# Channel-major matmuls that walk the tokens from the last to the first

## The chip, the cores and the metric

The kernel runs on one core of a Trainium2 chip. The metric is the device time of one execution in microseconds (us); before and after are timed in turn on the same chip. The engines are named as in the profile: PE is the matmul engine (TensorE), PEld its weight loads, DVE is VectorE, ACT is ScalarE, POOL is GpSimd, SP is the queue that issues most of the loads.

## What is computed

One layer of a hybrid encoder block on 256 tokens with 2048 channels, all in float32:

```
n = rms_norm(h, norm_mix_w)
proj = einsum("bsd,dp->bsp", n, w_in)          # 2048 -> 13344 channels
out_a = delta_mixer(...)                       # gated DeltaNet, both directions
out_b = dilated_mixer(...)                     # windowed attention, three dilations
h = h + einsum("bsm,md->bsd", concat(out_a, out_b), w_out)
n = rms_norm(h, norm_ffn_w)
up = depthwise_conv(einsum("bsd,df->bsf", n, w_ffn_in), conv_ffn_w)   # 2048 -> 11264
h = h + einsum("bsf,fd->bsd", silu(gate) * val, w_ffn_out)            # 5632 -> 2048
out = rms_norm(h, norm_final_w)
```

## The kernel before, in words

Nearly all the work is in four large matrix products. Each float32 weight is split into a rounded part `hi` (ACT, line 265) and a remainder `lo` (DVE, line 266), both of the type float32r, and the activations are kept in the same way as a pair. A product is then three matmuls that add into one bank of PSUM: hi by high, hi by low, lo by high. The weights come in pieces of 1 MB over SP's queue into four buffers (`raws`), are split into four buffers (`his`, `los`), and each split piece is one item of a list that `run_items` works off in order; the smaller work of the layer (convolutions, DeltaNet, attention) is dealt out between the items by `pump`.

Where a result is wanted with channels on the partitions and tokens along the row ("channel-major"), `cm_block` makes it: the query, key, value and z projections of DeltaNet, the queries and keys of attention, and the whole up projection of the MLP. The weights are the stationary operand, 128 x 128; the moving operand is a row of `xcat`, which for each of 16 groups of 128 channels holds 256 tokens of the high part and then 256 tokens of the low part, contiguous in SBUF. Each of the 168 blocks of 128 output channels makes 16 x 3 matmuls of 256 columns into columns 0 to 255 of one bank (lines 314, 315 and 316, 2688 matmuls each). When the last has finished, one instruction reads the bank: `evac` on ACT (line 329), or for the up projection a multiplication on DVE (line 1375).

The other large products use the activations as the stationary operand and the weights as the moving one: `v_slab` (lines 382 to 384, 256 columns) and `tm_group` for the two output projections (lines 1224 to 1226, 512 columns). They do not go through `cm_block`.

A few instructions elsewhere touch memory in another order than ascending and contiguous, and the rows below show them. `evac(natural(pad))` and lines 1203 and 1204 write with a step of four elements (16 bytes); line 1204 also reads one operand so. Line 861 reads 2048 elements of the tile `W` from the last to the first (steps of -64 and -1). Line 763, on POOL, runs four times for each head; two of the four write 64-element runs in descending order (the second and the third), the other two in ascending order.

Of the kernel before, what the change touches and what calls it, by code (L numbers as in the profile page):

```python
# [11 lines left out]
T = 256  # L12
D = 2048
KT = D // P
# [71 lines left out]
def block_kernel(tc, A, out, dbg=None):  # L86
# [7 lines left out]
    mm = nc.tensor.matmul  # L94
# [9 lines left out]
    def aview(t, off, dims):  # L104

        return bass.AP(tensor=t.tensor, offset=t.offset + off, ap=[list(t.ap[0])] + [list(d) for d in dims])
# [41 lines left out]
    xcat = xp.tile([P, KT, 512], F32R, name="xcat")  # L148
# [150 lines left out]
    def next_acc():  # L299
        accn[0] += 1  # L300
        return accs[accn[0] % len(accs)]

    def cm_block(ch, j, done, width=P):

        box = {}

        def half(kh):
            def mms(hi, lo):
                if kh == 0:
                    box["acc"] = next_acc()  # L310
                acc = box["acc"][:width, :T]
                for kk in range(8):
                    k = kh * 8 + kk
                    mm(acc, lhsT=hi[:, kk, :], rhs=xcat[:, k, :T], start=k == 0, stop=False)  # L314
                    mm(acc, lhsT=hi[:, kk, :], rhs=xcat[:, k, T:], start=False, stop=False)  # L315
                    mm(acc, lhsT=lo[:, kk, :], rhs=xcat[:, k, :T], start=False, stop=k == KT - 1)  # L316

            return mms

        for kh in range(2):  # L320
            Item(ch[kh], lambda t, j=j: t[:, :, j * width : (j + 1) * width], half(kh),
                 (lambda: done(box["acc"])) if kh else None, AT_CM)
# [129 lines left out]
    for k2 in range(8):  # L452
        bk = DB.get()
        for e in range(2):
            k = 2 * k2 + e
# [4 lines left out]
        for e in range(2):  # L460
            k = 2 * k2 + e
            src = bk[:, e * T : (e + 1) * T]
            ACT(xcat[:, k, :T], src, AF.Copy, scale=nw_mix[:, k : k + 1])
        for e in range(2):
            k = 2 * k2 + e
# [1019 lines left out]
```

## Time and profile before

| what | value |
|---|---|
| median of 3 runs | 1547.11 us (1544.25 to 1547.69) |
| the profiled execution, its own time | 1545.1 us |
| its span, first to last instruction | 1543.3 us |
| mean granted clock of PE | 0.997 of full speed |
| PE busy | 98% of the span |
| DVE, ACT, POOL busy | 67%, 54%, 11% |

The profile is of one execution. Its own time is 1.8 us above its span and 2.0 us below the median of the three runs.

### The profile page before, as it was taken

Reading aid. Unit: us, or ns where it says so; the run is one execution under the profiler, and the core shown is the slowest. Engines: PE = TensorE matmul, PEld = TensorE weight load, DVE = VectorE, ACT = ScalarE, POOL = GpSimd, SP = SyncE. Lnnn points to the kernel's source line nnn. Section 1 sums busy time; section 2 is a strip of 40 time slices with the busy share of each in tenths; the row PEclk is TensorE's granted clock in tenths of the full one; section 3 lists DMA queues with packets and bytes.
Section 4 is the critical chain, followed back from the end, with each engine's and each line's share of the span. In section 5 each row is a group of like instructions: output and inputs, shape, how many; then the busy total and the mean of one; then the engine's idle time right before and its main releaser. Section 6 shows DMA issues by size and latency. Waiting matters only on the chain.

```text
span 1543.3 us, 28173 instructions
## 1 busy us (share of the span) xinstructions
PE 1514.2 (98%) x11531; PEld 1443.4 (94%) x11531; DVE 1039.9 (67%) x1703; ACT 827.9 (54%) x1430; POOL 164.5 (11%) x245
## 2 busy tenths in 40 slices
PE   7999998999999999999999999999999999999997
PEld 7999998999999999997889999999999999888886
DVE  5878976979864666665557767677676676455454
ACT  5598874545555646554555544544544544344342
POOL 3264552000012202100000000000000000000000
PEclk9999999999999999999999999999999999999999
DMA  9656789646558636634765555565655657566552
GB/s 255 219 184 223 233 294 214 203 145 204 183 142 258 206 122 204 199 124 151 272 217 184 173 191 192 172 209 167 198 185 179 203 165 260 197 210 207 191 191 82
DMA packets 247283, 301.20 MB, mean 195 GB/s; under 512 B 10981, under 2 KB 207766, under 8 KB 246770
## 3 DMA queue, kind: packets, MB, share of 16 engines
q1 hardware_dynamic: 235602, 269.81, 54.4%
q0 software_dynamic: 11120, 29.01, 6.1%
q8 instruction: 90, 1.47, 0.4%
q10 hardware_dynamic: 432, 0.59, 0.1%
q14 instruction: 39, 0.32, 0.1%
HBM read 285.69 MB, written 13.65 MB: 194 GB/s over the span
## 4 chain that ended last, share of the span: by engine, by line
PE 91%; DMA 3%; ACT 2%; issue 2%; DVE 1%; POOL 1%; POOLq 0%; SPq 0%; ACTq 0%; DVEq 0%
PE bank L314 19%; PE bank L316 19%; PE bank L315 19%; PE bank L1224 7%; PE bank L1225 7%; PE bank L1226 7%; PE bank L382 3%; PE bank L383 3%; PE bank L384 3%; DMA raw<-in_w_in_dram 1%; PE bank L978 1%; PE bank L1024 1%; ACT hi L265 1%; PE bank L1019 1%; ACT kb L748 1%
## 5 line engine op out<-in xcount | busy, mean ns | idle before, releaser
L266 DVE TENSOR_TENSOR lo<-raw,hi 128x1024 fp32r<-128x1024 f32 x504 | 619.3, 1230 | 399.9 <-ACT hi L265 397.5
L265 ACT ACTIVATE hi<-raw 128x1024 fp32r<-128x1024 f32 x504 | 533.5, 1060 | 548.7 <-PE bank L315 262.5
L314 PE MATMUL bank<-xcat,hi 128*128 128x256 f32 x2688 | 758.4, 282 | 5.4 <-ACT qk L329 5.1
L315 PE MATMUL bank<-xcat,hi 128*128 128x256 f32 x2688 | 751.8, 280 | 0.0
L316 PE MATMUL bank<-xcat,lo 128*128 128x256 f32 x2688 | 751.6, 280 | 0.0
L314 PEld LDWEIGHTS bank<-xcat,hi 128*128 128x128 f32 x2688 | 506.2, 188 | 8.4 <-ACT qk L329 5.5
L315 PEld LDWEIGHTS bank<-xcat,hi 128*128 128x128 f32 x2688 | 512.0, 190 | 0.0
L316 PEld LDWEIGHTS bank<-xcat,lo 128*128 128x128 f32 x2688 | 505.6, 188 | 0.0
L1226 PE MATMUL bank<-hi,gtl 128*128 128x512 f32 x336 | 130.7, 389 | 0.0
L1225 PE MATMUL bank<-lo,gth 128*128 128x512 f32 x336 | 130.7, 389 | 0.0
L1224 PE MATMUL bank<-hi,gth 128*128 128x512 f32 x336 | 130.7, 389 | 0.0
L382 PE MATMUL bank<-hi,xcat 128*128 128x256 f32 x384 | 109.2, 284 | 0.0
L384 PE MATMUL bank<-hi,xcat 128*128 128x256 f32 x384 | 106.9, 278 | 0.0
L383 PE MATMUL bank<-lo,xcat 128*128 128x256 f32 x384 | 106.8, 278 | 0.0
L1224 PEld LDWEIGHTS bank<-hi,gth 128*128 128x128 f32 x336 | 63.1, 188 | 13.2
L1226 PEld LDWEIGHTS bank<-hi,gtl 128*128 128x128 f32 x336 | 63.1, 188 | 13.1
L1225 PEld LDWEIGHTS bank<-lo,gth 128*128 128x128 f32 x336 | 63.1, 188 | 13.0
L382 PEld LDWEIGHTS bank<-hi,xcat 128*128 128x128 f32 x384 | 72.4, 188 | 0.5
L384 PEld LDWEIGHTS bank<-hi,xcat 128*128 128x128 f32 x384 | 72.5, 189 | 0.0
L383 PEld LDWEIGHTS bank<-lo,xcat 128*128 128x128 f32 x384 | 72.3, 188 | 0.0
L1388 DVE SCALAR_TENSOR_TENSOR fy<-fpad,cwf,fy 128x256 f32<-128x256 f32 x132 | 63.4, 480 | 2.3
L1418 POOL DMA_DIRECT2D nfb<-in_norm_final_w_dram x1 | 0.6, 585 | 485.7 <-PE bank L316 485.7
(299 smaller groups left out, 1439.2 us busy)
## 6 DMA issues: line engine op xcount, KB each, us to landing
raw<-in_w_in_dram SPq DMA_DIRECT2D x104, 1024.0 KB, 5.7
raw<-in_w_ffn_in_dram SPq DMA_DIRECT2D x88, 1024.0 KB, 5.2
raw<-in_w_ffn_out_dram SPq DMA_DIRECT2D x44, 1024.0 KB, 5.0
raw<-in_w_out_dram SPq DMA_DIRECT2D x14, 1024.0 KB, 5.1
rec_d<-rec POOLq DMA_DIRECT2D x8, 768.0 KB, 7.1
rr<-rec_d POOLq DMA_DIRECT2D x6, 512.0 KB, 4.7
xt<-in_x_dram SPq DMA_DIRECT2D x4, 512.0 KB, 8.4
gam<-cg_d POOLq DMA_DIRECT2D x8, 256.0 KB, 8.7
```

Of the source, the lines that this page charges most:

```text
L265: ACT(hi, src, AF.Copy)
L266: V.tensor_sub(lo, src, hi.bitcast(F32))
L314: mm(acc, lhsT=hi[:, kk, :], rhs=xcat[:, k, :T], start=k == 0, stop=False)
L315: mm(acc, lhsT=hi[:, kk, :], rhs=xcat[:, k, T:], start=False, stop=False)
L316: mm(acc, lhsT=lo[:, kk, :], rhs=xcat[:, k, :T], start=False, stop=k == KT - 1)
L382: mm(o, lhsT=xh, rhs=hi[:, kk, :], start=k == 0 and t == 0, stop=False, skip_group_check=True)
L383: mm(o, lhsT=xh, rhs=lo[:, kk, :], start=False, stop=False, skip_group_check=True)
L384: mm(o, lhsT=xl, rhs=hi[:, kk, :], start=False, stop=k == KT - 1, skip_group_check=True)
L1224: mm(a[t], lhsT=xh, rhs=hi[:, kk, :], start=st, stop=False)
L1225: mm(a[t], lhsT=xh, rhs=lo[:, kk, :], start=False, stop=False)
L1226: mm(a[t], lhsT=xl, rhs=hi[:, kk, :], start=False, stop=sp_)
L1388: stt(y, pad[:, d : d + T], cwf[:, d, b : b + 1], y, op0=ALU.mult, op1=ALU.add)
```

## The change

In `cm_block` alone, both token axes are turned round. The accumulator's view starts at column 255 and steps by -1; the two views of `xcat` start at token 255 and step by -1. The moving operand is thus read from the last token to the first, and the sum is written from the last column to the first, so that each token still lands in its own column. `aview` builds an access pattern from a tile, an offset and pairs of step and count. The weights, the order of the three matmuls, the banks and the readers of the banks stay as they are. Two lines are added, so that all later line numbers grow by 2.

```
             def mms(hi, lo):
                 if kh == 0:
                     box["acc"] = next_acc()
-                acc = box["acc"][:width, :T]
+                acc = aview(box["acc"][:width], T - 1, [[-1, T]])
                 for kk in range(8):
+
                     k = kh * 8 + kk
-                    mm(acc, lhsT=hi[:, kk, :], rhs=xcat[:, k, :T], start=k == 0, stop=False)
-                    mm(acc, lhsT=hi[:, kk, :], rhs=xcat[:, k, T:], start=False, stop=False)
-                    mm(acc, lhsT=lo[:, kk, :], rhs=xcat[:, k, :T], start=False, stop=k == KT - 1)
+                    xh, xl = [aview(xcat[:, k, :], o + T - 1, [[-1, T]]) for o in (0, T)]
+                    mm(acc, lhsT=hi[:, kk, :], rhs=xh, start=k == 0, stop=False)
+                    mm(acc, lhsT=hi[:, kk, :], rhs=xl, start=False, stop=False)
+                    mm(acc, lhsT=lo[:, kk, :], rhs=xh, start=False, stop=k == KT - 1)
```

## Rows read from the trace of the kernel before

**Rows 1.** The page's first part: busy time, share, instructions of each engine.
```profile
PE 1514.2 (98%) x11531; PEld 1443.4 (94%) x11531; DVE 1039.9 (67%) x1703; ACT 827.9 (54%) x1430; POOL 164.5 (11%) x245
```

**Rows 2.** The page's fourth part: the chain that ended last, by engine and line.
```profile
PE 91%; DMA 3%; ACT 2%; issue 2%; DVE 1%; POOL 1%; POOLq 0%; SPq 0%; ACTq 0%; DVEq 0%
PE bank L314 19%; PE bank L316 19%; PE bank L315 19%; PE bank L1224 7%; PE bank L1225 7%; PE bank L1226 7%; PE bank L382 3%; PE bank L383 3%; PE bank L384 3%; DMA raw<-in_w_in_dram 1%; PE bank L978 1%; PE bank L1024 1%; ACT hi L265 1%; PE bank L1019 1%; ACT kb L748 1%
```

**Rows 3.** Matmuls by line and shape: count, busy us, mean ns, idle before.
```profile
L314 PE MATMUL bank<-xcat,hi 128*128 128x256 f32 x2688 | 758.4, 282 | 5.4 <-ACT qk L329 5.1 <-ACT pad L329 0.2
L315 PE MATMUL bank<-xcat,hi 128*128 128x256 f32 x2688 | 751.8, 280 | 0.0
L316 PE MATMUL bank<-xcat,lo 128*128 128x256 f32 x2688 | 751.6, 280 | 0.0
L1226 PE MATMUL bank<-hi,gtl 128*128 128x512 f32 x336 | 130.7, 389 | 0.0
...
L1198 PE MATMUL bank<-PT,vv 128*128 128x128 f32 x64 | 8.4, 275 | 0.0
...
L1195 PE MATMUL bank<-PT,vv 128*128 128x256 f32 x32 | 8.2, 378 | 0.0
```

**Rows 4.** Four stretches: length, busy us (count) of PE, PEld, DVE, ACT, POOL, PEclk, DMA.
```profile
346.00:384.00 38.00, 38.00 (x338) 38.00 (x337) 35.17 (x46) 21.86 (x35) 0.00 (x0) 1.00 0.66 209
900.00:938.00 38.00, 38.00 (x325) 38.00 (x325) 26.65 (x40) 19.80 (x29) 0.00 (x0) 1.00 0.62 201
1000.00:1100.00 100.00, 100.00 (x851) 100.00 (x851) 70.26 (x105) 49.41 (x70) 0.00 (x0) 1.00 0.58 190
1300.00:1400.00 100.00, 100.00 (x443) 82.81 (x442) 49.79 (x47) 41.74 (x43) 0.70 (x1) 1.00 0.64 216
```

**Rows 5.** ACT by line and shape: ascending, contiguous copies, and one with 16-byte steps.
```profile
L265 ACT ACTIVATE hi<-raw 128x1024 fp32r<-128x1024 f32 x504 | 533.5, 1060 | 548.7 <-PE bank L315 262.5 <-PE bank L1226 158.9 <-issue 63.8
...
L329 ACT ACTIVATE qk<-bank 128x256 f32<-128x256 f32 x48 | 17.8, 370 | 0.0
...
L329 ACT ACTIVATE pad<-bank 128x256 f32<-128x256 f32 x19 | 11.9, 624 | 0.1
...
L425 ACT ACTIVATE g_hi<-g_raw 128x512 fp32r<-128x512 f32 x1 | 0.6, 609 | 0.0
```

**Rows 6.** ACT's line 861, the descending read: ns min/median/max, first and last start.
```profile
L861 ACT ACTIVATE tm<-W x1: 1911/1911/1911, 449.8 to 449.8; 64x2048 f32<-64x2048 f32 x1
```

**Rows 7.** DVE by line and shape: a contiguous subtraction and one with 16-byte steps.
```profile
L1403 DVE TENSOR_TENSOR gtl<-fy,gth 128x256 fp32r<-128x256 f32 x22 | 9.1, 415 | 0.5 <-ACT gth L1402 0.5
...
L1204 DVE TENSOR_TENSOR mxl<-bank,mxh 128x256 fp32r<-128x256 f32 x8 | 5.1, 639 | 17.5 <-ACT mxh L1203 17.5
```

**Rows 8.** POOL's line 763 in four stretches: first ascending, second descending, twice.
```profile
101.20:101.70 0.50, 0.45 (x1) 1.00 0.49 51
101.70:102.25 0.55, 0.46 (x1) 1.00 0.82 136
202.00:202.51 0.51, 0.45 (x1) 1.00 1.11 353
202.51:203.10 0.59, 0.45 (x1) 1.00 1.15 356
```

**Rows 9.** DVE's line 1375, the reader of a bank in the up projection.
```profile
L1375 DVE TENSOR_TENSOR fpad<-bank,rC x88: 416/419/421, 814.5 to 1297.6; 128x256 f32<-128x256 f32 x88
```

## The prediction, made before the result

> **What bounds the kernel now.** I read the page's busy times first: PE is busy for 1514.2 of 1543.3 us, so that it stands still for 29 us in all [rows 1]. A busy PE is not yet a bound, so I then read the chain that ended last: 91% of it is PE, and the three lines that the change edits hold 19% each, 57% together [rows 2]. Nothing else in the kernel has as much weight, and no other engine is near its limit in the same stretches (DVE 70%, ACT 49% in the up projection [rows 4]).
>
> Next, how fast these matmuls follow each other. Their mean duration of 280 ns [rows 3] says little, since they overlap. The counts in a stretch say it: a matmul of 0.28 us that straddles an edge is counted too, so some 2.4 more are counted than start inside. From 1000 to 1100 us that makes 100 / (851 - 2.4) = 117.8 ns from one start to the next [rows 4]. From 1300 to 1400 us, where each matmul has 512 columns and lasts 389 ns, it is 100 / (443 - 1.7) = 226.6 ns [rows 3, 4]. [...] So 117.8 ns is 108.8 ns of streaming and 9 ns of fixed cost. PE has no gap between these matmuls: whatever the new order adds to a matmul of 256 columns, it adds to the end, 8064 times (3 x 2688 [rows 3]).
>
> One more thing must be read here. From 346 to 384 us the same three lines run at 38 / (338 - 2.4) = 113.2 ns [rows 4]: with the same shapes and the same buffers the engine has two gaits, 4.6 ns apart, and the up projection (88 blocks, 4224 matmuls) runs in the slower one, as 900 to 938 us shows, too.
>
> **The change part by part.** No instruction is added, removed or moved: there are as many matmuls, weight loads, copies and DMAs, in the same order, with the same waits. The weight loads are as before. The readers of the bank read the same columns after the same last matmul, 419 ns on DVE [rows 9]; they cost what they did. What is left is two changes of direction in 8064 instructions, the read of the moving operand and the write of the sum. No matmul before reads or writes downward, so each is bounded from both sides.
>
> The read. What another order can cost shows on other engines: ACT takes 624 instead of 370 ns for 256 elements when it writes each 16 bytes apart, 1.0 ns an element more [rows 5]; DVE, which writes and reads one operand so, takes 639 instead of 415 ns, 0.88 ns an element more [rows 7]. The price of jumping is thus there to be seen. The price of going backward is not: ACT reads 2048 elements downward in 1911 ns [rows 6]; from 512 elements in 609 ns and 1024 in 1060 ns, upward, a line through both gives 1962 ns for 2048 [rows 5]. POOL's downward writes take 0.46 and 0.45 us where its upward ones take 0.45 and 0.45 [rows 8]. So a step of -1 is no jump, on the one engine that reads fast enough to tell (0.83 ns an element). PE reads twice as fast, 0.425 ns, and there no row decides. Lower bound 0 ns a column, upper bound another 0.425 ns, as if the columns went singly and no longer two in the time of one of ACT's elements. The nearest rows are ACT's, so I take 0.
>
> The write. No row shows a matmul that writes PSUM other than upward, and none shows another engine that writes PSUM. What the rows do have is matmuls in plain float32, whose columns come slower: 378 ns for 256 columns against 275 ns for 128 [rows 3], 0.80 ns a column. So PE does have a gait of half the column rate, 0.38 ns a column more. Lower bound 0, upper bound 0.38 to 0.425 ns; POOL's writes, the nearest that go downward, say 0, and I take 0 with less confidence than for the read, because POOL needs 3.5 ns for an element (0.45 us for 128) and could hide much.
>
> [...]
>
> The sum: 8064 x 256 x 0 = 0 us against the profiled execution's 1545.1 us. The median of the three runs shown is 2.0 us higher, and I forecast between the two, **1546 us**, no change that can be told: a difference under 0.2% (3 us) is about what this measurement cannot tell from none, the three runs being 0.22% apart themselves.
>
> **The rivals.**
>
> *Half rate.* Read or write lose the pairing of columns, each column takes twice its 0.425 ns, and a matmul of 256 columns comes to cost what one of 512 does, 226.6 ns. That is 8064 x 108.8 ns = 877 us; by the plain float32 rows it is 8064 x 256 x 0.38 ns = 784 us. PE's own 29 us of standing still can cover a little, since its suppliers would be earlier. It gives 1545 + 784 - 29 = 2300 us to 1545 + 877 = 2422 us, most likely near 2400. Place: every cm_block matmul; it decides as soon as a column costs more than 0.425 ns, since nothing on PE hides it. For it: PE's columns are twice as fast as any engine's elements in these rows, so something must deliver two at a time, and that may be built for upward order. Against it: the downward read on ACT at full rate. [...]
>
> *A jump for every column.* A step of -1 costs what a 16-byte jump costs, 0.88 to 1.0 ns: 8064 x 256 x 0.88 = 1817 us and more, 3360 us or later. Rows 6 speak against it plainly for the read.
>
> *A little more for each matmul.* A stream that starts at the far end of a line could need a few more ns to begin, or the up projection's gait could fall another step. One step of 4.6 ns in the up projection's 4224 matmuls is 19 us, in all 8064 it is 37 us; a doubled fixed cost of 9 ns is 73 us. It gives 1565 to 1620 us. For it: the gait does depend on something other than the shape [rows 4].
>
> *The other gait.* If the new order lets the up projection run at 113.2 ns, 4224 x 4.6 ns = 19 us go, and the time is 1526 us. For it: the faster gait is there, 38 us long, with the same instructions. Against it: nothing in the change touches the weight loads or the first columns' distance from the matmul before.
>
> *Nothing is turned round.* As read and write are reversed together, the product is the same as before; if the two were undone on the way to the chip, the time would be 1546 us as well, and time alone would not tell it from my forecast.
>
> **How the numbers follow.** No cost, with nothing turned round in it: 0.56. Half rate: 0.22. A jump for every column: 0.04. A little more for each matmul: 0.10. The other gait: 0.08, taking in whatever lands just below. So faster by over 0.2% has 0.08, within 0.2% 0.56, slower by over 0.2% 0.22 + 0.04 + 0.10 = 0.36. The likeliest case alone would lie between 1541 and 1552 us. Leaving out no more than 2 in 10 forces the range up through the half rate: from 1540 to 2425 us it leaves out the other gait and the jump, 0.12. The middle of it, 1630 to 2290 us, is not expected at all.
>
> **What the profile after would show.** If I am right, the three lines (316, 317 and 318 then) keep 2688 instructions each and a mean of 280 to 282 ns, the stretch from 1000 to 1100 us holds about 851 matmuls again, and PE stays at 98%. Half rate would show in the same place: about 443 matmuls in 100 us, means near 390 ns, DVE and ACT falling to half their share, while lines 382 to 384 and 1224 to 1226 (384 to 386 and 1226 to 1228 then) keep theirs. A lost pairing on the read only and one on the write only look alike there; they would have to be told apart by turning one alone. A changed gait shows as 113 or 122 ns between starts, with everything else alike. Wrong I would be if PE's moving read or its write into PSUM takes two columns at a time only when they come in rising order, which ACT at one element at a time cannot show.

## The result, and the profile after

The changed kernel takes 1555.37 us (median of 4 runs, 1553.83 to 1556.43), against 1547.4 us before (4 runs): a ratio of 1.0053, with a 95% interval from 1.0038 to 1.0069. It is slower by 8.0 us. I had forecast no change. The profiled execution took 1553.83 us, with a span of 1552.0 us.

The page of the changed kernel, its first part, and under it the chain that ended last. They answer to [rows 1] and [rows 2]:

```profile
PE 1526.4 (98%) x11531; PEld 1456.2 (94%) x11531; DVE 1041.4 (67%) x1703; ACT 828.4 (53%) x1430; POOL 162.3 (10%) x245
...
PE 93%; DMA 3%; issue 2%; DVE 1%; ACT 1%; POOL 1%; POOLq 0%; SPq 0%; ACTq 0%; DVEq 0%
PE bank L316 19%; PE bank L317 19%; PE bank L318 19%; PE bank L1226 7%; PE bank L1227 7%; PE bank L1228 7%; PE bank L384 3%; PE bank L385 3%; PE bank L386 3%; DMA raw<-in_w_in_dram 1%; PE bank L980 1%; PE bank L1026 1%; PE bank L1021 1%; DMA xt<-in_x_dram 0%; DMA Bt<-a_d 0%
```

The same instructions, the same chain. PE is busy for 12.2 us more and stands still for 1552.0 - 1526.4 = 25.6 us where it was 29.1: the work became longer and a part of its waits shorter.

The changed lines by line and shape, as in [rows 3]:

```profile
L316 PE MATMUL bank<-xcat,hi 128*128 128x256 f32 x2688 | 764.7, 284 | 4.0 <-ACT qk L331 4.0
L317 PE MATMUL bank<-xcat,hi 128*128 128x256 f32 x2688 | 758.1, 282 | 0.0
L318 PE MATMUL bank<-xcat,lo 128*128 128x256 f32 x2688 | 753.7, 280 | 0.0
```

The mean duration has hardly moved and, as before, says little. The stretches do (columns as in [rows 4]); first the changed kernel, with one stretch more than [rows 4] has, and then the kernel before in that stretch:

```profile
300.00:400.00 100.00, 100.00 (x846) 99.59 (x845) 81.31 (x119) 53.38 (x83) 0.00 (x0) 1.00 0.53 166
346.00:384.00 38.00, 38.00 (x323) 37.90 (x322) 32.87 (x43) 19.44 (x29) 0.00 (x0) 1.00 0.53 167
900.00:938.00 38.00, 38.00 (x325) 38.00 (x324) 26.80 (x42) 19.66 (x28) 0.00 (x0) 1.00 0.62 202
1000.00:1100.00 100.00, 100.00 (x852) 100.00 (x851) 71.49 (x107) 50.42 (x73) 0.00 (x0) 1.00 0.58 189
```

```profile
300.00:400.00 100.00, 100.00 (x867) 99.58 (x866) 83.06 (x123) 53.33 (x81) 0.00 (x0) 1.00 0.56 176
```

In these two stretches of the up projection nothing has changed: 325 and 852 matmuls, 117.8 ns from one start to the next. But the stretch from 346 to 384 us, which ran at 113.2 ns [rows 4], now holds 323 matmuls in place of 338, and the longer stretch around it 846 in place of 867. The granted clock is 1.00 in all of them.

Where the 8.7 us of span lie can be read from two lines: the first of the changed matmul lines, and the DVE line that reads the bank in the up projection (durations in ns, first and last start; in [rows 9] it is 814.5 to 1297.6):

```profile
L316 PE MATMUL bank<-xcat,hi x2688: 278/282/415, 26.2 to 1303.6; 128*128 128x256 f32 x192
```

```profile
L1377 DVE TENSOR_TENSOR fpad<-bank,rC x88: 418/419/422, 823.3 to 1306.3; 128x256 f32<-128x256 f32 x88
```

From the first of these readers to the last it is 483.0 us, and 483.1 before; from there to the end 245.7 us in both. So everything is lost before the first reader. I took the start of every matmul of the three lines from the timeline. The first of them starts at 26.2 us and not at 25.1, which is 1.1 us; one of the kernels below starts as late and is not slower. From the first to the 3840th, the last one ahead of the up projection, 634.1 us pass now, and 626.7 before: 7.4 us. Of the 639 groups of six successive starts in those stages, 351 were 113.3 ns apart before and 142 were 117.8; the other 146 hold a wait or another instruction. After, no group is at 113.3. The 351 take 10.0 us more (342 of them are at 117.8 ns now, eight at 120), the 142 take 0.4 us more, and the 146 take 3.0 us less: 7.4 us.

Another 0.6 us was lost in the first 120 matmuls of the up projection, and 0.3 us was won just ahead of it; that makes the 8.7 us. The up projection comes in items, list entries of 24 matmuls each, and the first five of them take 15.5 us now and 14.9 before. Before, they too ran at 113.3 ns, but for a few matmuls behind each interruption. Then line 1298 puts four small matmuls between the fifth and the sixth item (at 811.4 us), and the 4104 matmuls behind them follow each other at 117.8 ns. Two stretches of the kernel before, 5 us long, one on either side, with 47 and 45 matmuls:

```profile
806.30:811.30 5.00, 5.00 (x47) 5.00 (x46) 3.62 (x12) 2.67 (x4) 0.71 (x1) 1.00 0.67 213
816.00:821.00 5.00, 5.00 (x45) 5.00 (x44) 3.64 (x6) 2.20 (x4) 0.00 (x0) 1.00 0.00 0
```

So the streams that had found the faster gait have lost it, and the long stream of the up projection, which had been in the slower one from the sixth item on, lost nothing. The experiments ask which of the two directions does that, whether the price is one per matmul, and what it would be if the up projection had been in the faster gait.

### The profile page after: what moved, and what is told of

It is laid out like the page before. It is cut to its first block, busy times and chain, and to the rows that moved or that the text cites. A ratio compares the mean times of both kernels' runs of the same rounds, so it can differ in the third digit from the quotient of the medians.

```text
span 1552.0 us, 28173 instructions
## 1 busy us (share of the span) xinstructions
PE 1526.4 (98%) x11531; PEld 1456.2 (94%) x11531; DVE 1041.4 (67%) x1703; ACT 828.4 (53%) x1430; POOL 162.3 (10%) x245
## 4 chain that ended last, share of the span: by engine, by line
PE 93%; DMA 3%; issue 2%; DVE 1%; ACT 1%; POOL 1%; POOLq 0%; SPq 0%; ACTq 0%; DVEq 0%
PE bank L316 19%; PE bank L317 19%; PE bank L318 19%; PE bank L1226 7%; PE bank L1227 7%; PE bank L1228 7%; PE bank L384 3%; PE bank L385 3%; PE bank L386 3%; DMA raw<-in_w_in_dram 1%; PE bank L980 1%; PE bank L1026 1%; PE bank L1021 1%; DMA xt<-in_x_dram 0%; DMA Bt<-a_d 0%
```

## Experiments

**The price by itself.** A kernel that leaves the layer out and only repeats streams of 36 matmuls, with the write and the read turned one at a time and both, and with the read started a few elements further on.

> This kernel leaves out the whole layer and measures the disputed cost alone: twelve variants of one stream of 36 float32r matmuls (weights reloaded for each), each stream begun eight times, after 1 to 8 plain float32 transposes; 256 columns in ten variants (read and write up or down in the four combinations, the read begun 1, 2 or 3 elements later, the write begun 2 elements later, the downward read begun 1 or 2 elements later), 512 columns up and down in two. Theory A, the gait: an upward stream settles at its start at 113.3 or at 117.8 ns from one matmul to the next, and a downward one only at 117.8; so the upward variant shows some of its eight streams at 113.3, the downward one none. Theory B, a cost for each matmul: the downward variant is about 1.1 ns slower (8.5 us over 8064 matmuls) than the upward one in every stream. Theory C, chance: which gait a stream takes has nothing to do with the direction, and both variants show both gaits.

The timeline has one row for a stream (start, duration of the stream): up and up, both down, write up and read down, write down and read up, read started one element further; then 512 columns, up and down.

```profile
24.53 4.55 PE L146 MATMUL bank<-mov,wei 128*128 128x256 f32 x36
...
62.86 4.50 PE L146 MATMUL bank<-mov,wei 128*128 128x256 f32 x36
...
100.90 4.50 PE L146 MATMUL bank<-mov,wei 128*128 128x256 f32 x36
...
139.03 4.55 PE L146 MATMUL bank<-mov,wei 128*128 128x256 f32 x36
...
177.67 4.66 PE L146 MATMUL bank<-mov,wei 128*128 128x256 f32 x36
...
407.70 8.46 PE L146 MATMUL bank<-mov,wei 128*128 128x512 f32 x36
...
477.44 8.65 PE L146 MATMUL bank<-mov,wei 128*128 128x512 f32 x36
```

Less the last matmul (0.28 us) and over 35 intervals, 4.55 us are 122.0 ns and 4.50 are 120.6. These means take in the slower first starts of each stream; from the tenth start on it is 120.0 and 118.4 ns. The write's direction makes no difference (4.55 us both ways with the read upward, 4.50 with it downward), the read's does, but here downward is the *faster* one, and a start one element (4 bytes) further on costs more (125.1 ns, 123.0 from the tenth start on) than turning round. At 512 columns it is the other way, 5 ns a matmul more downward ((8.65 - 8.46) / 35; 226.8 and 233.3 ns from the tenth start on). No stream of the bench settles at 113.3 or 117.8 ns, the kernel's gaits, and theory B has the wrong sign here. With the read two elements further on, the eight upward streams settle at 116.7, 120.0 or 126.7 ns, although they differ in the number of transposes ahead alone. So in this bench the spacing changes with how a stream starts (116.7 to 126.7 ns in that variant) and with where the read begins (120.0 ns, and 123.0 one element on), and at its addresses, which are not the kernel's, it shows neither of the kernel's gaits and doesn't price the kernel's matmuls.

**Only the read, only the write, only the up projection.** Three kernels that do a part of the change each. Against the changed kernel, the first turns the write back, the second the read, and the third does both only where `rev` is set, which the up projection's call alone does:

```
-                acc = aview(box["acc"][:width], T - 1, [[-1, T]])
+                acc = box["acc"][:width, :T]
```

```
-                    xh, xl = [aview(xcat[:, k, :], o + T - 1, [[-1, T]]) for o in (0, T)]
+                    xh, xl = [xcat[:, k, o : o + T] for o in (0, T)]
```

```
-                acc = aview(box["acc"][:width], T - 1, [[-1, T]])
+                acc = aview(box["acc"][:width], T - 1, [[-1, T]]) if rev else box["acc"][:width, :T]
...
-                    xh, xl = [aview(xcat[:, k, :], o + T - 1, [[-1, T]]) for o in (0, T)]
+                    xh, xl = [aview(xcat[:, k, :], o + T - 1, [[-1, T]]) if rev else xcat[:, k, o : o + T] for o in (0, T)]
```

> Only the moving operand is read from the last token to the first, the sum is written upward, so that the tokens of these products come out in reversed order. If the read is what costs (theory A or B), the time is that of the change, about 1555 us, and in the stretch around 360 us the channel-major matmuls follow each other at 117.8 ns. If the write is what costs, it is about 1547 us with stretches at 113.3 ns, as before. If each has a part (theory B), it lies between, near 1551 us.

> Only the sum is written from the last column to the first, the moving operand is read upward; the tokens of these products come out in reversed order. The complement of the run before: about 1555 us without any stretch at 113.3 ns if the write is what costs, about 1547 us with such stretches if the read is.

> Read and write are turned round in the up projection alone (4224 of 8064 matmuls). Theory A: the up projection ran at 117.8 ns already, so nothing is lost there: 1547 us, within 0.2% of before, and its stretches count 851 matmuls in 100 us as before. Theory B: 4224 x 1.05 ns = 4.4 us more, about 1551.5 us. Theory C: any of the gaits, so 1528 or 1547 us.

The last three were timed beside the kernel before at 1547.43 us (21 runs):

| turned round | median, us | ratio to before, 95% interval |
|---|---|---|
| both (the change) | 1555.37 | 1.0053 [1.0038, 1.0069] |
| the read alone | 1553.82 | 1.0046 [1.0029, 1.0062] |
| the write alone | 1547.52 | 1.0001 [0.9988, 1.0014] |
| both, in the up projection alone | 1547.9 | 1.0008 [0.9999, 1.0018] |

The stretches of the kernel with the read alone, of that with the write alone, and of that with the up projection alone:

```profile
346.00:384.00 38.00, 38.00 (x323) 37.90 (x321) 32.83 (x43) 19.45 (x29) 0.00 (x0) 1.00 0.55 167
...
1000.00:1100.00 100.00, 100.00 (x851) 100.00 (x850) 70.99 (x107) 49.88 (x72) 0.00 (x0) 1.00 0.58 188
```

```profile
346.00:384.00 38.00, 38.00 (x338) 38.00 (x337) 35.14 (x46) 21.86 (x35) 0.00 (x0) 1.00 0.68 208
...
1000.00:1100.00 100.00, 100.00 (x851) 100.00 (x851) 71.07 (x107) 49.51 (x70) 0.00 (x0) 1.00 0.57 185
```

```profile
346.00:384.00 38.00, 38.00 (x336) 37.96 (x335) 33.36 (x44) 20.62 (x32) 0.00 (x0) 1.00 0.64 194
...
1000.00:1100.00 100.00, 100.00 (x851) 100.00 (x850) 70.22 (x106) 50.22 (x71) 0.00 (x0) 1.00 0.58 188
```

The read carries it all: 323 matmuls with it and 338 without, and no group of six at 113.3 ns with the read alone (374 groups with the write alone, 376 with the up projection alone). The up projection holds 851 in 100 us whichever way its operands run, so its half of the change cost nothing that the time can tell; its first five items take 15.5 us, as in the changed kernel. This last kernel starts its first matmul of the three lines at 26.1 us, as late as the changed one.

**At the kernel's own addresses.** A bench again without the layer: `xcat`, weights and banks lie where the kernel has them, and the weights start at 13 offsets from 0 to 128 elements, each offset with streams of 48 matmuls upward and downward, after 1, 2 and 8 small transposes. A second one goes downward through all offsets from 0 to 63, after 2 and 8.

> This kernel leaves out the layer again: only streams of 48 channel-major matmuls as the kernel makes them (hi by high, hi by low, lo by high), with hi, lo and xcat at the same addresses in SBUF as in the kernel and nothing beside PE at work. The weights begin at 0, 4, 8, 16, 24, 32, 40, 48, 64, 80, 96, 112 or 128 elements from the start of their buffers (the kernel has 32), each with an upward and a downward read and write, each stream begun three times (after 1, 2 and 8 transposes). The bench before gave 122.0 ns from start to start upward and 120.6 downward, but 119.1 to 128 for the upward read begun 1 to 3 elements later, so that the place of the operands counts. Theory D, places: which of two directions is faster depends on where the weights lie against the moving row; at 32 upward is the faster one (113.3 against 117.8), at some other offset downward is as fast as upward at its best. Theory A, direction: downward never goes below 117.8 at any offset, upward reaches 113.3 at some.

> As x5_bench_places, the layer left out, downward streams alone, and the weights begin at each of 0 to 63 elements (x5 showed a period of 64: the offsets 32 and 96, 0, 64 and 128, 48 and 112 gave the same). Each stream is begun twice, after 2 and after 8 transposes. In x5 upward reached 113.3 ns at 32 and 96 alone; downward had 117.8 to 120 ns at every offset tried. Theory D, places: some offset among the 64 gives downward 113.3 ns as well, and the change would then cost nothing with the weights there. Theory A, direction: no offset gives downward less than 117.8.

The timeline of the first bench at offset 32, after 8 transposes. Two starts of the upward stream, 30 matmuls apart, and then two of the downward one, 30 apart as well:

```profile
217.01 0.28 PE L139 MATMUL bank<-xcat,hi 128*128 128x256 f32 x1
...
220.41 0.28 PE L139 MATMUL bank<-xcat,hi 128*128 128x256 f32 x1
...
235.14 0.28 PE L139 MATMUL bank<-xcat,hi 128*128 128x256 f32 x1
...
238.67 0.28 PE L139 MATMUL bank<-xcat,hi 128*128 128x256 f32 x1
```

3.40 / 30 = 113.3 ns upward, 3.53 / 30 = 117.7 ns downward: the kernel's two gaits. Upward 113.3 ns comes at offsets 32 and 96 alone, after 2 and 8 transposes; after one it is 117.8 ns at 32 and 96, too. At the eleven other offsets upward streams take 116.7 to 120 ns, and those of the 13 that lie 64 elements apart agree (0, 64 and 128; 16 and 80; 32 and 96; 48 and 112). Downward none of the 64 offsets gives less than 117.7 ns (117.7 to 120.0). The first stream of each of the two benches, with starts 333 ns apart, is left out. Downward has more than one gait, too: at offset 32 it is 120.0 ns after one transpose. And downward is not the slower direction everywhere: at 16 and 80 it takes 118.3 or 118.4 ns where upward takes 120.0, at 24 it takes 117.8 where upward takes 118.5 or 120.0. So which direction is faster depends on the place in these two benches, as theory D has it; but 113.3 ns was to be had upward alone, and there at two of 13 offsets, after 2 and 8 transposes and not after one.

**Starting the up projection anew.** If the start decides, a few small transposes ahead of the up projection's long stream should put it into the faster gait, upward alone. Two and then eight of them were put behind line 1298, between the fifth and the sixth item, into the kernel before and into the changed one:

```
+            bk = yield from take(SB)
+            for _ in range(2):     # 8 in the second pair
+                nc.tensor.transpose(bk[:, :P], ident, ident)
+            SB.put(bk)
```

> The kernel before (upward), with two transposes into a spare bank after line 1298, right ahead of the up projection's one long stream of matmuls; their result is not used. In x5 the upward stream with the weights at 32 took 117.8 ns after one transpose and 113.3 after two or eight. Theory A or D, a gait settled at the start of a stream: the up projection falls into 113.3 ns, some 4100 x 4.5 ns = 18 us less, 1529 us; its stretches of 100 us hold 885 matmuls and not 851. Theory E, the up projection's gait comes from what runs beside it: it stays at 117.8, 1547 us.

> The changed kernel with the same two transposes. If a downward stream with the weights at 32 has no gait below 117.8, the transposes bring nothing: 1555 us, and then the price of the change against the kernel before with its transposes is 26 us, 1.7%, and no longer 8. If a downward stream only needs another start, it gains as the upward one does: 1537 us.

The upward expectation missed. Two transposes: 1546.94 us upward (0.9998 [0.9987, 1.0009]) and 1553.42 us downward (1.0036 [1.0023, 1.0049]); the up projection kept 851 matmuls in 100 us. To see which starts do work, the next kernel, upward, puts 1 to 8 transposes ahead of each of 24 items of the up projection, from the ninth on, in `run_items`:

```
+            for _ in range(kicks.get(i, 0)):
+                nc.tensor.transpose(banks[7][:, :P], ident, ident)
```

> The kernel before (upward); ahead of 24 items near the beginning of the up projection, 1 to 8 transposes into a bank that nobody reads, so that the stream begins anew 24 times there; afterwards it runs on undisturbed. The starts themselves cost about 24 x 0.6 us = 14 us. If the gait is settled at each start, some of the 24 items of 24 matmuls run at 113.3 ns and others at 117.8, and the long rest keeps whatever the last start gave: 1562 us with the rest at 117.8, about 1545 with it at 113.3. If the up projection's slower gait comes from what runs beside it, all 24 run at 117.8, 1562 us.

1542.58 us, 0.9975 [0.9963, 0.9987]. By the starts in the timeline, all 12 items behind 5 or more transposes ran at 113.3 ns (the next expectation counts thirteen), of the 12 behind 1 to 4 four ran at 113.3 and eight at 117.8, and the 3480 matmuls behind the last of the starts (8 transposes, 896 us) stayed in the faster gait to the end:

```profile
900.00:938.00 38.00, 38.00 (x338) 38.00 (x337) 28.17 (x43) 19.47 (x28) 0.00 (x0) 1.00 0.64 209
1000.00:1100.00 100.00, 100.00 (x884) 100.00 (x884) 73.11 (x111) 52.10 (x74) 0.00 (x0) 1.00 0.61 198
```

> The kernel before (upward) with eight transposes, and not two as in x7, right ahead of the up projection's long stream. In x9 all thirteen starts after five or more transposes gave 113.3 ns, and the stream of 3480 matmuls after the last one kept it to its end. If that holds for one start alone, the up projection loses 4100 x 4.5 ns = 18 us and pays under 1 us for the transposes: 1529 us, 885 matmuls in each 100 us. If several starts are needed, 1547.

> The changed kernel with the same eight transposes. If the downward read has no gait below 117.8 ns, nothing is gained: 1555 to 1556 us, and the price of the direction, both kernels started alike, is 26 us or 1.7%. If it gains as the upward one does, 1537 us, and the direction costs only in the w_in products.

Eight transposes at the first place missed again: 1547.87 us upward (1.0012 [1.0000, 1.0025]), 851 matmuls in 100 us; downward 1555.94 us (1.0064 [1.0047, 1.0082]). The place in the upward kernel, and its stretch:

```profile
811.56 0.28 PE L316 MATMUL bank<-xcat,lo 128*128 128x256 f32 x1
811.67 0.60 PE L1298 MATMUL bank<-cst,ss 128*128 128x128 f32 x4
812.11 1.04 PE L1303 MATMUL bank<-cst 128*128 128x128 f32 x8
812.91 0.36 PE L314 MATMUL bank<-xcat,hi 128*128 128x256 f32 x1
...
1000.00:1100.00 100.00, 100.00 (x851) 100.00 (x850) 69.86 (x105) 50.57 (x72) 0.00 (x0) 1.00 0.59 190
```

With the four matmuls of line 1298, twelve small ones stand between the fifth and the sixth item here, and six in the kernel with two transposes. So "five or more" is not enough, and neither is a start between two items, which this place is as well: the stream that ends there had run at 113.3 ns, and the next one runs at 117.8, as in the kernel before. So the last pair takes the starts where they had worked, two of them, 8 transposes each, ahead of the 13th and the 25th item of the up projection (`kicks.update({n_out + 12: 8, n_out + 24: 8})`, where `n_out` items come ahead of the up projection), in the kernel before and in the changed one:

> The kernel before (upward) with eight transposes ahead of two items of the up projection, the 13th and the 25th after the output projection, as in x9, but only these two. In x9 all starts between two items after five or more transposes gave 113.3 ns; in x10 eight transposes right after line 1298 did not. If a start between two items is what counts, the up projection runs at 113.3 ns from the first of them on: some 3750 x 4.5 ns = 17 us less for 2 us of transposes, 1531 us. If x9 owed it to its many starts, 1549 us.

> The changed kernel with the same two starts. If the downward read has no gait below 117.8 ns, 1557 us, and the direction is worth 26 us between two kernels started alike; if it follows the upward one, 1539 us.

Upward 1531.51 us, 0.9896 [0.9879, 0.9913]; downward 1556.32 us, 1.0058 [1.0038, 1.0078]. The stretches, first upward and then downward:

```profile
900.00:938.00 38.00, 38.00 (x338) 38.00 (x337) 27.74 (x43) 19.80 (x28) 0.00 (x0) 1.00 0.57 181
1000.00:1100.00 100.00, 100.00 (x885) 100.00 (x884) 72.48 (x111) 51.60 (x73) 0.00 (x0) 1.00 0.59 191
```

```profile
900.00:938.00 38.00, 38.00 (x325) 38.00 (x324) 26.82 (x41) 19.04 (x27) 0.00 (x0) 1.00 0.62 200
1000.00:1100.00 100.00, 100.00 (x852) 100.00 (x851) 70.64 (x107) 49.83 (x71) 0.00 (x0) 1.00 0.59 190
```

885 matmuls against 852. Upward, 16 transposes of no use to the result take 15.5 us off the kernel before, timed beside it at 1547.03 us, and this version beats both kernels; downward the same 16 give nothing back. The first eight were enough for the gait: the twelve items between the two starts are at 113.3 ns already. Between the two kernels lie 24.8 us: that is what the change costs when both get these starts, three times what it showed without them. That it is the read's here, too, is carried over from the runs that turn one direction alone.

## Why the prediction was wrong

**The step that failed** is "The read": "The nearest rows are ACT's, so I take 0." The cost is not 0. ACT's row [rows 6] does say that its descending read is no jump (1911 ns for 2048 elements), and the runs agree for PE's: nothing near 0.425 ns a column was paid, which is the distance of 226.6 ns at 512 columns less 117.8 at 256 [rows 4], over 256 columns. But the price, 4.5 ns in 113, is 0.018 ns for each of 256 columns, and the line through ACT's upward rows missed its downward one by 51 ns in 1911: such a row could not show it. The working priced the read per column, and multiplied by 8064 matmuls; the runs showed a price in the gait, paid by the 2100 matmuls or so that had been in the faster one (10.0 us ahead of the up projection, less 3.0 us of waits that became shorter). I had both gaits before me [rows 4], and used them for rivals without asking what keeps a stream in the faster one; and I took all 4224 matmuls of the up projection to run in the slower one, where the first 120 did not.

**The write** at 0 was right: 1.0001 [0.9988, 1.0014] with the write alone. The streams that write downward hold 338 and 851 matmuls in their stretches, as before [rows 4].

**The parts that stayed.** Counts, readers and weight loads are as said: 2688 instructions a line, 419 ns for the reader, the up projection at 851 or 852 in 100 us. That last number I had named as the sign that I was right, and it held while the time moved: I looked for the sign in the stage with the most matmuls, of which all but the first five items already ran in the slower gait and had nothing to lose. Of my signs, "a changed gait" was the one that came, at 346 to 384 us.

**The rivals.** *Half rate* and *a jump for every column* did not occur in any run. That PE takes columns in pairs and ACT elements singly was my reading of 0.425 ns a column against 0.83 an element, and no run shows a pairing; nor does any run show that two directions at half rate would cost 108.8 ns a matmul only once, as the sum to 2422 us has it: the read alone cost 0.46% of the time and the write alone 0.01%. *A little more for each matmul* is nearest in size but not in mechanism: it had one step more for each matmul of the up projection, 19 us, and none was taken there but in its first five items (0.6 us). It is a step up for the 2100 matmuls ahead of it that were in the faster gait. *The other gait* had the right mechanism and the wrong sign for this change: the up projection can run at 113.3 ns, and gives back 15.5 us of the 19 that I worked out when it does, but upward. Downward it did not in any of six kernels that read so there. *Nothing is turned round* falls with the read alone.

**What stays open.** Why the downward read excludes the faster gait, inside PE or in its reads of SBUF, no run shows. Direction and place are not wholly apart either: a downward read also begins at another element, token 255 in place of 0. The benches at the kernel's addresses moved the weights alone, and the first bench shows that moving the start of the read changes the spacing; whether a downward read that begins elsewhere finds 113.3 ns was not tried. Nor is it settled what lets an upward stream find it: 5 or more transposes ahead of an item did in all 12 cases from the ninth item on, and 8 did in both of the last pair's upward starts; 2 and 8 behind line 1298 did not, between two items as well. And why upward streams of the bench reached 113.3 ns with the weights at two of 13 offsets, no run explains.

## What to carry to other kernels

Read the distance from start to start in every stage, not in the largest one alone: where the same instruction shows two distances (here 113.3 and 117.8 ns), a change can take the faster one away (351 groups of six had it before, none after), and a stage already in the slower one can hide the price (851 matmuls in 100 us before, 852 after). A cost read from one engine's rows says nothing of a price smaller than those rows can show: here ACT's line missed its downward row by 51 ns in 1911, 2.7%, and the price was 0.018 ns a column. And before PE's long streams of equal matmuls are called bound, it is worth a run to break a slow one with a few small transposes: here 16 of them took 1.0% off a kernel in which PE is busy for 98% of the span, while 2 and 8 at another place did nothing.

## What the runs showed of the hardware

In these kernels a gait, once found, held for thousands of matmuls: 4104 at 117.8 ns before, 3480 at 113.3 ns with the starts, with loads, copies and waits of other engines going on beside them. With the place of the operands and the start of a stream the distance between matmuls of 256 columns, once settled, went from 113.3 to 123.0 ns in the rows above (126.7 in one other variant of the first bench), at a granted clock of 1.00; a read 4 bytes further on moved it by 3 ns, from 120.0 to 123.0. Offsets of the weights 64 elements (256 bytes) apart gave the same distances where both were tried, 113.3 ns upward at 32 and at 96, 120.0 at 16 and at 80. The direction of the write to PSUM moved nothing in the two runs that turn it alone (120.0 ns either way in the first bench, 1.0001 [0.9988, 1.0014] for the kernel).
